# A two-block transformer kernel on one core: the modulation products in wider steps at fixed places, and an attention bias table kept as rows

## The chip, the cores and the metric

The kernel runs on one core of a Trainium2 chip. The core has a matrix engine (TensorE, PE in the profile; its weight loads are PEld), VectorE (DVE), ScalarE (ACT), GpSimd (POOL) and SyncE (SP), which here issues every DMA from one queue, in order. The metric is device time in microseconds for one execution.

## The reference, cut to what matters

`first_block` has two layers. Each takes a vector `mod = silu(c) @ w_ada[li] + b_ada[li]` of 6 x 1024 numbers for the tokens, and the same for the context from `c_ctx`. It is split into a shift, a scale and a gate for the mixer, and a shift, a scale and a gate for the feed-forward part:

```python
m  = unpack(modulate(rms_norm(x, norm1_w[li]), sh1, sc1) @ w_in[li], lb_all[li])
...
x = x + g1 * merge(att, rec, four, w_out[li], dt)
x = x + g2 * conv_ffn(modulate(rms_norm(x, norm2_w[li]), sh2, sc2),
                      w_up[li], conv_w[li], conv_b[li], w_down[li])
```

`second_block` is a gated convolution and then an attention over three groups of heads, with a bias that depends on the distance alone, `bias = bias_tab[bucket]`, in windows of 128 queries by 256 keys:

```python
logits = jnp.where(valid, logits + bias, -jnp.inf)
```

There are 256 tokens and 256 context tokens of width 1024, all in float32.

## The kernel before, in words

Every large product is made of three matmuls per 128 rows of the contraction, on numbers split into a high and a low part. A weight block of 256 columns is fetched as two DMAs of 512 KB into tiles `raw` (`wpart`, L136), rounded to its high part by ScalarE (L138) and to its low part by VectorE (L140). There are three `raw` buffers and two pairs of weight tiles. `gemm` (L160) then forms one product of 128 columns, 24 matmuls over 256 or 512 tokens; `gemm_nat` (L171) forms the transposed kind, 24 matmuls over 256 columns.

The stages follow one another: the start; layer 0's mixer (a gated scan `hgrn`, two halves of an attention `diff_attn`, a Fourier part); its out-projection with `w_out_a` and `w_out_b`; layer 0's feed-forward block (`ffn`: twice 11 pairs of products, then 8 products down), on 512 columns since tokens and context both go on; layer 1 on 256; then the second block.

The modulation vector is wanted in 12 pieces of 1024 columns (banks). The first two of layer 0, the shift and scale of its mixer, are formed at the start. For the other ten, `ada_bank` fetches, for each of eight parts of the contraction, a tile `araw` of 4 x 256 columns (512 KB, L316) and runs four float32 matmuls, each into its own quarter of 32 of the array's columns (L319, 128*32 in the profile). A float32 matmul shows as two records. At the end of a bank `ada_out` copies the sums out, transposes them with PE (L330) and adds the bias. There are three `araw` buffers. The order is not written out by hand: the framework's scheduler places each instruction by a priority, and the table `_ADA` gives each bank an offset by which it stands behind the rest, so that its matmuls fill places where the scheduler finds nothing else:

```python
for a, off in _ADA[li]:
    with self.tc.high_priority(offset=-off):
        self.ada_bank(*a)
```

At the beginning of layer 0's feed-forward block `bias_tables` makes the attention's bias. For each of five window kinds a small matmul (L883) gives, per head, 256 numbers over distance. A DMA (L886) writes them to DRAM as 128 windows of 128, each shifted by one and running backwards: 16 heads x 128 windows x 512 bytes, 1 MB. The attention later reads one head's five windows as a contiguous tile `bt` of 320 KB (L1016). VectorE adds it to the scores (L1136). The query rows are scaled at L1114, and the head outputs leave at L1164.

Of the kernel before, what the change touches and what calls it, by code (L numbers as in the profile page):

```python
# [46 lines left out]
for _n, _w in (("hsel", 32), ("bsel", 512), ("low", 1)):  # L47
# [5 lines left out]
_ADA = ((((0, 2), 800), ((0, 3), 1000), ((0, 4), 1300), ((0, 5), LATER), ((1, 0), LATER), ((1, 1), LATER)),  # L53
        (((1, 2), 500), ((1, 3), 700), ((1, 4), 1200), ((1, 5), LATER)))

# [3 lines left out]
class Builder:  # L59
# [4 lines left out]
    gi = 0  # L64
    keep = {}
# [65 lines left out]
    def wpart(self, W, src, a, b, hold=(None, None)):  # L131
# [4 lines left out]
        nc.sync.dma_start(raw, src.rearrange("p (k c) -> p k c", k=H.shape[1])[:, a:b])  # L136
# [14 lines left out]
    def gemm(self, W, c0, acts, T, t0=0, pt=None, tag=None):  # L151
# [6 lines left out]
        for k, (h, l) in enumerate(acts):  # L158
            for a, c in ((H, h), (H, l), (L, h)):
                nc.tensor.matmul(pt, a[:, k, c0:c0 + P], c[:, t0:t0 + T], start=n == 0, stop=n == tot - 1)  # L160
                n += 1
        return pt

    def gemm_nat(self, W, acts, t0, pt, p0):
# [143 lines left out]
    def ada_bank(self, li, b):  # L308
# [5 lines left out]
        for k in range(KD):  # L314
            raw = self.ring("araw", [P, 4, 256])
            nc.sync.dma_start(raw, d["w_ada"][li, k * P:(k + 1) * P, b * 1024:(b + 1) * 1024]  # L316
                              .rearrange("p (g c) -> p g c", g=4))
            for g in range(4):
                nc.tensor.matmul(pa[32 * g:32 * g + 32, 0:256], self.csil[:, k, :], raw[:, g],  # L319
                                 start=k == 0, stop=k == KD - 1)  # L320
        self.ada_out(li, pa, [b * 8 + g * 2 for g in range(4)], 2)

    def ada_out(self, li, pa, tiles, n):

        nc, mod = self.nc, self.mods[li]
        ad = self.ring("araw", [P, 512])
# [186 lines left out]
    def layer(self, li, states):  # L513
# [29 lines left out]
        for a, off in _ADA[li]:  # L543
            with self.tc.high_priority(offset=-off):
                self.ada_bank(*a)
# [78 lines left out]
        a0 = rec(0, "ps")  # L624
        values()
# [25 lines left out]


# [145 lines left out]
    def ffn(self, li, st2, T):  # L798
# [15 lines left out]
        if li == 0:  # L814
            with self.later():
                self.bias_tables()
        st1 = [dict() for _ in range(ns)]
        hook = self.out_hook(st1[0]) if li == 1 else None
        for half in range(2):
            hid = []  # L820
            for j in range(half * HALF, (half + 1) * HALF):
                w = pre[j] if j in pre else self.wload(d["w_up"][li, j])
# [39 lines left out]
            if cut < 8:  # L862
                ws = [W(m) for m in (6, 7)]
                for v in (1, 0):
                    for m in (6, 7):
                        add(m, v, self.gemm(ws[m - 6], 0, hid, 256, t0=v * 256))
        return st1


    def bias_tables(self):  # L870
# [3 lines left out]
        self.scr = self.dp.tile([16, P, 5, P], F32, name="scr")  # L874
# [5 lines left out]
        for b in range(5):  # L880
# [111 lines left out]
    def attn2(self, st, acts, x):  # L992
# [378 lines left out]
```

## Time and profile before

| | |
|---|---|
| median of three runs | 1778.97 us (1778.38 to 1779.42) |
| profiled execution, its own time | 1775.45 us |
| span of the profiled execution | 1773.6 us |
| mean granted TensorE clock | 0.987 |
| PE busy | 1707.7 us, 96% |
| VectorE, ScalarE, GpSimd busy | 57%, 48%, 18% |
| DMA | 260.64 MB, 147 GB/s on the mean |

The span runs from the first to the last instruction of the profiled execution, and the execution's own time is 1.85 us longer. A busy PE is not one at its peak: a matmul's record includes the time it takes to run out of the array, so that overlapping records are counted once, and a short piece between others carries that time alone. A wait stands in square brackets behind the instruction that followed it, with what ended it.

### The profile page before, as it was taken

The page shows a single profiled execution, that of the slowest core. Times are in us where ns is not written, and L with a number is a line of the kernel's source. Part 1 is how long each engine was busy: PE and PEld are TensorE (multiplying, and loading weights), DVE is VectorE, ACT ScalarE, POOL GpSimd, SP SyncE. Part 2 cuts the span into 40 slices and gives each one's busy share as a digit, 9 for nine tenths or more (in the row PEclk, how much of TensorE's full clock was granted, in tenths as well). Part 3 has the DMA queues.
Part 4 walks back from the last instruction along what each step waited for, and adds up shares of the span by engine and source line. Part 5 has one row for each costly group of instructions (what it writes and reads, how often), then busy time and mean ns, then how long its engine had stood idle before and what let it go on. Part 6 is the DMA issues. An engine that isn't in the chain of part 4 may idle for free.

```text
span 1773.6 us, 29835 instructions
## 1 busy us (share of the span) xinstructions
PE 1707.7 (96%) x11918; PEld 1462.1 (82%) x11918; DVE 1018.5 (57%) x1849; ACT 846.3 (48%) x1481; POOL 320.8 (18%) x412
## 2 busy tenths in 40 slices
PE   6999999987999999989999899999999999999998
PEld 3876766765878888779787799999999999899987
DVE  4557555444543454355865676767666754645656
ACT  4447444334431343253754554665444565545543
POOL 1322210121100011225320210122202203121220
PEclk9999999998999999989999999999999999999999
DMA  9533443576223222344326556555555555444441
GB/s 344 174 108 107 133 133 126 148 125 174 101 69 132 100 95 71 119 150 133 106 86 215 174 165 197 177 176 181 182 185 187 175 186 168 150 142 148 150 144 44
DMA packets 88803, 260.64 MB, mean 147 GB/s; under 512 B 8887, under 2 KB 20535, under 8 KB 88664
## 3 DMA queue, kind: packets, MB, share of 16 engines
q1 hardware_dynamic: 88664, 258.74, 45.6%
q8 instruction: 93, 1.52, 0.3%
q14 instruction: 46, 0.38, 0.1%
HBM read 252.42 MB, written 6.29 MB: 146 GB/s over the span
## 4 chain that ended last, share of the span: by engine, by line
PE 88%; DVE 3%; DMA 3%; ACT 2%; SPq 2%; issue 1%; POOL 0%; ACTq 0%; DVEq 0%
PE pg L160 35%; PE ps L160 15%; PE pu L160 8%; PE ph L160 8%; PE pg L171 7%; PE pa L319 3%; DMA araw<-in_w_ada_dram 2%; PE ps L1129 2%; PE ph L442 1%; PE ps L698 1%; PE pa L1159 1%; PE ph L1155 1%; SPq L316 1%; DVE wL L140 1%; PE pu L736 1%
## 5 line engine op out<-in xcount | busy, mean ns | idle before, releaser
L140 DVE TENSOR_TENSOR wL<-raw,wH 128x1024 fp32r<-128x1024 f32 (+2 forms) x388 | 443.0, 1171 | 254.3 <-ACT wH L138 247.6
L138 ACT CAST wH<-raw 128x1024 fp32r<-128x1024 f32 (+2 forms) x388 | 370.9, 994 | 406.3 <-PE pg L160 157.7
L160 PE MATMUL pg<-hx,wH 128*128 128x256 f32 x1152 | 215.0, 284 | 0.0
L160 PE MATMUL pg<-hm,wH 128*128 128x512 f32 (+1 forms) x736 | 209.7, 366 | 2.8 <-DVE x L657 1.8
L160 PEld LDWEIGHTS pg<-hx,wH 128*128 128x128 f32 x1152 | 178.6, 189 | 5.3 <-issue 4.0
L160 PEld LDWEIGHTS pg<-hm,wH 128*128 128x128 f32 x736 | 130.1, 192 | 42.3 <-issue 13.3
L160 PE MATMUL pg<-hx,wL 128*128 128x256 f32 x576 | 163.1, 283 | 0.0
L160 PE MATMUL pg<-hm,wL 128*128 128x512 f32 (+1 forms) x368 | 132.5, 361 | 0.0
L160 PE MATMUL pg<-h,wH 128*128 128x256 f32 (+1 forms) x464 | 116.1, 339 | 13.2 <-ACT wH L138 11.6
L843 POOL TENSOR_TENSOR tt<-tt 128x512 f32<-128x512 f32 (+1 forms) x44 | 44.7, 1017 | 442.1 <-DVE tt L840 442.1
L160 PE MATMUL ps<-h,wH 128*128 128x256 f32 (+1 forms) x464 | 114.6, 335 | 0.0
L160 PEld LDWEIGHTS pg<-hx,wL 128*128 128x128 f32 x576 | 108.2, 188 | 0.7 <-issue 0.2
L160 PEld LDWEIGHTS pg<-h,wH 128*128 128x128 f32 x464 | 80.7, 193 | 24.0 <-ACT wH L138 12.0
L160 PEld LDWEIGHTS ps<-h,wH 128*128 128x128 f32 x464 | 80.3, 191 | 9.4
L160 PE MATMUL pg<-hid,wH 128*128 128x256 f32 (+1 forms) x360 | 81.6, 318 | 1.1 <-ACT wH L138 1.1
L160 PEld LDWEIGHTS pg<-hm,wL 128*128 128x128 f32 x368 | 70.6, 192 | 14.0 <-issue 5.0
L160 PE MATMUL pg<-h,wL 128*128 128x256 f32 (+1 forms) x232 | 78.2, 337 | 0.0
L160 PE MATMUL ps<-hid,wH 128*128 128x256 f32 (+1 forms) x344 | 78.2, 319 | 0.0
L160 PE MATMUL ps<-h,wL 128*128 128x256 f32 (+1 forms) x232 | 77.6, 334 | 0.0
L319 PE MATMUL pa<-araw,csil 128*32 128x256 f32 x640 | 64.0, 401 | 13.1 <-DMA araw<-in_w_ada_dram 11.5
L187 POOL TENSOR_TENSOR acc<-acc,y 128x256 f32<-128x256 f32 x40 | 37.4, 944 | 205.0 <-ACT y L186 192.9
L160 PE MATMUL pu<-h,wH 128*128 128x256 f32 (+1 forms) x272 | 68.2, 336 | 6.0 <-ACT wH L138 6.0
(408 smaller groups left out, 3866.1 us busy)
## 6 DMA issues: line engine op xcount, KB each, us to landing
raw<-in_w_up_dram SPq DMA_DIRECT2D x88, 512.0 KB, 4.7
araw<-in_w_ada_dram SPq DMA_DIRECT2D x80, 512.0 KB, 5.3
raw<-in_attn_w_in_dram SPq DMA_DIRECT2D x80, 512.0 KB, 4.5
raw<-in_conv_w_in_dram SPq DMA_DIRECT2D x64, 512.0 KB, 4.6
raw<-in_w_in_dram SPq DMA_DIRECT2D x48, 512.0 KB, 4.6
raw<-in_w_down_dram SPq DMA_DIRECT2D x32, 384.0 KB, 3.6
raw<-in_w_down_dram SPq DMA_DIRECT2D x32, 320.0 KB, 2.9
raw<-in_conv_w_out_dram SPq DMA_DIRECT2D x16, 512.0 KB, 4.2
```

Source lines behind the costliest of these rows:

```text
L138: nc.scalar.copy(H[:, a:b], raw)
L140: nc.vector.tensor_tensor(L[:, a:b], raw, H[:, a:b].bitcast(F32), OP.subtract)
L160: nc.tensor.matmul(pt, a[:, k, c0:c0 + P], c[:, t0:t0 + T], start=n == 0, stop=n == tot - 1)
L171: nc.tensor.matmul(pt[:, p0:p0 + 256], c[:, t0:t0 + P], a[:, k, :], start=n == 0, stop=n == tot - 1)
L187: st["last"] = i, (nc.vector if last else nc.gpsimd).tensor_tensor(st["acc"], st["acc"], sq, OP.add)
L316: nc.sync.dma_start(raw, d["w_ada"][li, k * P:(k + 1) * P, b * 1024:(b + 1) * 1024] .rearrange("p (g c) -> p g c", g=4))
L319: nc.tensor.matmul(pa[32 * g:32 * g + 32, 0:256], self.csil[:, k, :], raw[:, g], start=k == 0, stop=k == KD - 1)
L442: nc.tensor.matmul(pt[:, v, c:c + P], l, m, start=True, stop=True)
L698: nc.tensor.matmul(pts[i][:, :n], qa[h][rr, qt * P:(qt + 1) * P], kT[h][rr, k0 * P:k0 * P + n], start=True, stop=True)
L736: nc.tensor.matmul(po[:, 0:P], aT[:, b * P:(b + 1) * P], va[kb // 2][:, kb % 2, hh * P:(hh + 1) * P], start=b == 0, stop=b == nk - 1)
L843: nc.gpsimd.tensor_tensor(tt[1], tt[0], tt[1], OP.mult)
L1129: nc.tensor.matmul(ps[v][:, o:o + ks.stop - ks.start], qh[g][rr[v], i, qs], kh[g][rr[v], i, ks], start=True, stop=True)
```

## The change

The ten later banks are formed in pairs as steps of 2048 columns. A step fetches two `araw` tiles of 2 x 512 columns and runs four matmuls of 512 columns, one per quarter. There are five pairs with eight steps each, 40 steps in place of 80. A step no longer has a low priority. `gemm` and `gemm_nat` call `tick`, and a step is put behind the product that it counts to: behind each product in layer 0's mixer after the first scan's inputs (the pairs 2 and 4 of layer 0), behind each second product in its feed-forward block from the third weight pair on (the pairs 0 and 2 of layer 1), behind each second in layer 1's mixer (pair 4). Each `araw` load is issued behind the latest weight load in the program's order.

The bias table is kept as 16 rows of 5 x 256 numbers, written by one DMA of 80 KB. The shifted windows are made when a tile is read, as 640 runs of 512 bytes that overlap in DRAM. They are not reversed any more. Instead the query rows are written in reversed order in each block of 128, and the head outputs are read reversed.

```diff
-_ADA = ((((0, 2), 800), ((0, 3), 1000), ((0, 4), 1300), ((0, 5), LATER), ((1, 0), LATER), ((1, 1), LATER)),
-        (((1, 2), 500), ((1, 3), 700), ((1, 4), 1200), ((1, 5), LATER)))
...
     def wpart(self, W, src, a, b, hold=(None, None)):
...
-        nc.sync.dma_start(raw, src.rearrange("p (k c) -> p k c", k=H.shape[1])[:, a:b])
+        self.fetch = nc.sync.dma_start(raw, src.rearrange("p (k c) -> p k c", k=H.shape[1])[:, a:b])
...
     def gemm(self, W, c0, acts, T, t0=0, pt=None, tag=None):
...
+        self.tick()
         return pt
...
     def gemm_nat(self, W, acts, t0, pt, p0):
...
+        self.tick()
...
-    def ada_bank(self, li, b):
+    def ada_steps(self, li, b):
...
         for k in range(KD):
-            raw = self.ring("araw", [P, 4, 256])
-            nc.sync.dma_start(raw, d["w_ada"][li, k * P:(k + 1) * P, b * 1024:(b + 1) * 1024]
-                              .rearrange("p (g c) -> p g c", g=4))
+            raw = [self.araw([P, 2, 512]) for _ in range(2)]
+            for i in range(2):
+                c = (b + i) * 1024
+                with self.after(self.fetch):
+                    nc.sync.dma_start(raw[i], d["w_ada"][li, k * P:(k + 1) * P, c:c + 1024]
+                                      .rearrange("p (g c) -> p g c", g=2))
             for g in range(4):
-                nc.tensor.matmul(pa[32 * g:32 * g + 32, 0:256], self.csil[:, k, :], raw[:, g],
+                nc.tensor.matmul(pa[32 * g:32 * g + 32, :], self.csil[:, k, :], raw[g // 2][:, g % 2],
                                  start=k == 0, stop=k == KD - 1)
-        self.ada_out(li, pa, [b * 8 + g * 2 for g in range(4)], 2)
+            if k == KD - 1:
+                self.ada_out(li, pa, [b * 8 + g * 4 for g in range(4)], 4)
+            yield
+
+    def araw(self, shape):
+        return self.lp.tile(shape, F32, name="araw", tag="araw", bufs=3)
+
+    def beside(self, banks, every):
+        self.steps = [self.ada_steps(*b) for b in banks]
+        self.every, self.count = every, 0
+
+    def tick(self):
+        self.count += 1
+        if self.steps and self.count % self.every == 0:
+            self.step()
...
+    def finish_steps(self):
+        while self.steps:
+            self.step()
...
         a0 = rec(0, "ps")
+        self.beside(((0, 2), (0, 4)) if li == 0 else ((1, 4),), 1 if li == 0 else 2)
...
             for j in range(half * HALF, (half + 1) * HALF):
+                if li == 0 and j == 2:
+                    self.beside(((1, 0), (1, 2)), 2)
...
-        self.scr = self.dp.tile([16, P, 5, P], F32, name="scr")
+        self.scr = self.dp.tile([16, 5, 256], F32, name="scr")
...
             nc.scalar.copy(bv[:, b], pt[0:16, 0:256])
-            src = bv[:, b]
-            nc.sync.dma_start(self.scr[:, :, b], bass.AP(tensor=src.tensor, offset=src.offset + 127,
-                                                         ap=[list(src.ap[0]), [-1, P], [1, P]]))
+        nc.sync.dma_start(self.scr, bv)
+
+    def reverse(self, t):
+        n = t.shape[-1] // P
+        return bass.AP(tensor=t.tensor, offset=t.offset + P - 1, ap=[list(t.ap[0]), [P, n], [-1, P]])
...
-            nc.sync.dma_start(t, self.scr[head])
+            row = self.scr[head]
+            nc.sync.dma_start(t, bass.AP(tensor=row.tensor, offset=row.offset, ap=[[1, P], [256, 5], [1, P]]))
```

Four places in the order of instructions follow. Lines of the changed kernel stand some way off: L134 is the weight load, L158 and L170 the products, L320 and L323 the modulation's loads and matmuls, L919 the bias write.

SP's queue around the start of layer 0's feed-forward block, before:

```order
L316 DMA araw<-in_w_ada_dram 128x1024
L886 DMA scr<-bt 2048x1x128
L136 DMA raw<-in_w_up_dram 128x1024
L316 DMA araw<-in_w_ada_dram 128x1024 x5
L886 DMA scr<-bt 2048x1x128 x3
L136 DMA raw<-in_w_up_dram 128x1024
L886 DMA scr<-bt 2048x1x128
L316 DMA araw<-in_w_ada_dram 128x1024 x3
L136 DMA raw<-in_w_up_dram 128x1024 x16
```

and now:

```order
L134 DMA raw<-in_w_up_dram 128x1024 x3
L912 DMA bt<-in_oh_dram 33x1280
L134 DMA raw<-in_w_up_dram 128x1024 x3
L320 DMA araw<-in_w_ada_dram 128x1024 x2
L919 DMA scr<-bt 16x1280
L134 DMA raw<-in_w_up_dram 128x1024 x2
L320 DMA araw<-in_w_ada_dram 128x1024 x2
L134 DMA raw<-in_w_up_dram 128x1024 x2
```

The five writes of 2048 runs, with modulation loads between them, are now one write of 16 rows. The first two loads of the steps that go into the block stand ahead of it.

PE at the end of the out-projection (products `pg<-hm`) and the start of the feed-forward block (`ph<-h`), before:

```order
L160 MATMUL pg<-hm,wL 128x256
L319 MATMUL pa<-araw,csil 32x256 x4
L210 MATMUL pg<-dg,ca 128x128 x2
L883 MATMUL pg<-bt,rb 16x256
L319 MATMUL pa<-araw,csil 32x256 x4
L192 MATMUL ps<-ca,acc 128x1 x2
L883 MATMUL ps<-bt,rb 16x256
L319 MATMUL pa<-araw,csil 32x256 x4
L883 MATMUL pg<-bt,rb 16x256
L319 MATMUL pa<-araw,csil 32x256 x4
L160 MATMUL ph<-h_3431,wH 128x256
L883 MATMUL ps<-bt,rb 16x256
```

and now:

```order
L158 MATMUL pg<-hm,wH 128x256 x2
L158 MATMUL pg<-hm,wL 128x256
L210 MATMUL pg<-dg,ca 128x128 x2
L917 MATMUL pg<-bt,rb 16x256 x2
L192 MATMUL ps<-ca,acc 128x1 x2
L158 MATMUL ph<-h_3230,wH 128x256
L158 MATMUL pg<-h_3230,wH 128x256
L917 MATMUL ps<-bt,rb 16x256 x2
L158 MATMUL ph<-h_3231,wH 128x256
L158 MATMUL ph<-h_3230,wL 128x256
```

The modulation's matmuls between the norm's sums (L192), the spread of its factor (L210) and the bias matmuls have left this place.

PE in layer 0's mixer, where values are formed from the weights `wH` and `wL` by `gemm_nat` (`pg<-wH,hm`, `pg<-wL,hm`), now:

```order
L170 MATMUL pg<-wH,hm 128x256 x2
L170 MATMUL pg<-wL,hm 128x256
L170 MATMUL pg<-wH,hm 128x256
L323 MATMUL pa<-araw,csil 32x512 x2
L170 MATMUL pg<-wH,hm 128x256
L170 MATMUL pg<-wL,hm 128x256
L170 MATMUL pg<-wH,hm 128x256
L323 MATMUL pa<-araw,csil 32x512 x2
```

A step of four matmuls stands here as two pieces of two, three product matmuls apart, since its two tiles are loaded separately.

PE in the feed-forward block, at the end of one weight block's second product (`ph`) and the start of the next, now:

```order
L158 MATMUL ph<-h_3245,wH 128x512
L158 MATMUL ph<-h_3244,wL 128x512
L323 MATMUL pa<-araw,csil 32x512 x4
L158 MATMUL pg<-h_3230,wH 128x512
L158 MATMUL pg<-h_3231,wH 128x512
L158 MATMUL pg<-h_3230,wL 128x512
L158 MATMUL pg<-h_3232,wH 128x512
```

One whole step stands between the products; before, they followed each other directly.

## Rows read from the trace of the kernel before

**Rows 1.** Busy time by engine, from the page: us, share of the span, instructions.

```profile
PE 1707.7 (96%) x11918; PEld 1462.1 (82%) x11918; DVE 1018.5 (57%) x1849; ACT 846.3 (48%) x1481; POOL 320.8 (18%) x412
```

**Rows 2.** Stretches: us, busy us of PE, PEld, DVE, ACT, POOL; clock, DMA share, GB/s.

```profile
45.00:330.00 285.00, 280.80 (x1793) 202.96 (x1792) 162.87 (x377) 145.86 (x322) 55.98 (x82) 1.00 0.39 128
...
424.00:765.00 341.00, 341.00 (x1546) 275.12 (x1544) 158.22 (x211) 120.57 (x169) 37.99 (x31) 1.00 0.30 100
...
800.00:990.00 190.00, 184.46 (x1348) 147.92 (x1346) 121.40 (x264) 99.95 (x202) 48.27 (x74) 1.00 0.44 144
```

**Rows 3.** Chain of waits, layer 0's feed-forward block: start, us, what.

```profile
430.15 5.60 PE ph L160 x24
```

**Rows 4.** Timeline of PE around modulation steps: start, us, instruction, records.

```profile
155.52 1.50 PE L319 MATMUL pa<-araw,csil 128*32 128x256 f32 x24
...
334.32 0.40 PE L160 MATMUL pg<-Qp,wL 128*128 128x512 f32 x1
...
334.64 0.64 PE L319 MATMUL pa<-araw,csil 128*32 128x256 f32 x8
...
335.21 0.51 PE L160 MATMUL pg<-hm,wH 128*128 128x256 f32 x2
...
335.56 0.29 PE L160 MATMUL pg<-hm,wL 128*128 128x256 f32 x1
```

**Rows 5.** Timeline of SP's queue at the start of the feed-forward block.

```profile
365.03 16.86 SPq L886 DMA_DIRECT2D scr<-bt  x3
...
381.94 12.60 SPq L136 DMA_DIRECT2D raw<-in_w_up_dram  x1
...
414.31 10.69 SPq L136 DMA_DIRECT2D raw<-in_w_up_dram  x5
```

**Rows 6.** DMA issues from 335 to 425 us, and two of the stretches there.

```profile
araw<-in_w_ada_dram SPq DMA_DIRECT2D x11, 512.0 KB, 7.2
...
scr<-bt SPq DMA_DIRECT2D x5, 1024.0 KB, 20.1
...
387.00:394.00 7.00, 7.00 (x49) 6.17 (x47) 0.00 (x0) 0.00 (x0) 0.00 (x0) 1.00 0.75 90
...
401.00:408.00 7.00, 2.34 (x5) 1.42 (x6) 2.36 (x3) 3.45 (x4) 0.00 (x0) 0.50 0.83 158
```

**Rows 7.** Timeline of PE at the start of the feed-forward block.

```profile
405.62 1.22 PE L160 MATMUL pg<-h,wH 128*128 128x512 f32 x2 [11.56 <-ACT wH L138]
...
409.69 0.63 PE L160 MATMUL pg<-h,wH 128*128 128x512 f32 x2
...
422.20 1.22 PE L160 MATMUL pu<-h,wH 128*128 128x512 f32 x2 [6.05 <-ACT wH L138]
...
426.49 0.63 PE L160 MATMUL pu<-h,wH 128*128 128x512 f32 x2
```

**Rows 8.** Timeline of PE between out-projection and feed-forward block.

```profile
358.06 1.08 PE L319 MATMUL pa<-araw,csil 128*32 128x256 f32 x8 [4.78 <-DMA araw<-in_w_ada_dram]
...
362.32 0.71 PE L210 MATMUL pg<-dg,ca 128*128 128x128 f32 x4
...
366.89 0.38 PE L160 MATMUL ph<-h,wH 128*128 128x256 f32 x1
```

**Rows 9.** Chain, transposed products in layer 1; DMA issues, 45 to 130 us.

```profile
798.47 20.16 PE pg L171 x171
...
araw<-in_w_ada_dram SPq DMA_DIRECT2D x9, 512.0 KB, 5.8
```

**Rows 10.** Timeline of VectorE at the start of layer 1.

```profile
771.10 0.16 DVE L200 RECIPROCAL rs<-sd 128x2 f32<-128x2 f32 x1
```

**Rows 11.** Bias tiles in the attention: DMA issues, SP's queue, first use on VectorE.

```profile
bt<-scr SPq DMA_DIRECT2D x13, 320.0 KB, 3.0
...
1524.89 2.79 SPq L1016 DMA_DIRECT2D bt<-scr  x2
...
1530.01 0.66 DVE L1136 CUSTOM_DVE_ANT_0 lt<-ps,bt 128x512 f32<-128x512 f32 x1
```

More of the change, by code (lines that the diff above doesn't have):

```diff
@@ L64 @@
     gi = 0
+    steps, every, count = (), 1, 0
     keep = {}
@@ L314, in ada_bank, with step @@
         for k in range(KD):
-            raw = self.ring("araw", [P, 4, 256])
-            nc.sync.dma_start(raw, d["w_ada"][li, k * P:(k + 1) * P, b * 1024:(b + 1) * 1024]
-                              .rearrange("p (g c) -> p g c", g=4))
+            raw = [self.araw([P, 2, 512]) for _ in range(2)]
[4 more added lines that the diff above has]
+                                      .rearrange("p (g c) -> p g c", g=2))
             for g in range(4):
-                nc.tensor.matmul(pa[32 * g:32 * g + 32, 0:256], self.csil[:, k, :], raw[:, g],
+                nc.tensor.matmul(pa[32 * g:32 * g + 32, :], self.csil[:, k, :], raw[g // 2][:, g % 2],
                                  start=k == 0, stop=k == KD - 1)
-        self.ada_out(li, pa, [b * 8 + g * 2 for g in range(4)], 2)
+            if k == KD - 1:
[10 more added lines that the diff above has]
+            self.step()
+    def step(self):
+        while self.steps:
+            try:
+                next(self.steps[0])
+                return
+            except StopIteration:
+                self.steps.pop(0)
+    def finish_steps(self):
+        while self.steps:
+            self.step()
     def ada_out(self, li, pa, tiles, n):
         nc, mod = self.nc, self.mods[li]
-        ad = self.ring("araw", [P, 512])
+        ad = self.araw([P, 512])
         nc.scalar.copy(ad[:, :n * P], pa[:, :n * P])
@@ L542, in layer @@
             self.late_setup()
-        for a, off in _ADA[li]:
-            with self.tc.high_priority(offset=-off):
-                self.ada_bank(*a)
         acts = h
@@ L650, in layer @@
         self.fourier(li, uf, T, mo, fc)
+        self.finish_steps()
         st2 = [dict() for _ in range(ns)]
@@ L815, in ffn @@
             with self.later():
-                self.bias_tables()
+                self.bias_rows()
         st1 = [dict() for _ in range(ns)]
@@ L866, in ffn, with bias_rows @@
                         add(m, v, self.gemm(ws[m - 6], 0, hid, 256, t0=v * 256))
+        self.finish_steps()
         return st1
-    def bias_tables(self):
+    def bias_rows(self):
         nc, d = self.nc, self.d
-        self.scr = self.dp.tile([16, P, 5, P], F32, name="scr")
+        self.scr = self.dp.tile([16, 5, 256], F32, name="scr")
         rb = self.sml("rb", [33, 48], bufs=1)
@@ L1113, in attn2 @@
                     o = self.ring(name, [P, 2, 256])
-                    nc.vector.scalar_tensor_tensor(o.rearrange("p i t -> p (i t)"), raw[n].rearrange("p i t -> p (i t)"),
-                                                   gain, pc, op0=OP.mult, op1=OP.mult)
+                    f = o.rearrange("p i t -> p (i t)")
+                    blocks = lambda t: t.rearrange("p (n t) -> p n t", t=P)
+                    nc.vector.scalar_tensor_tensor(blocks(f) if n else self.reverse(f),
+                                                   blocks(raw[n].rearrange("p i t -> p (i t)")),
+                                                   gain, blocks(pc), op0=OP.mult, op1=OP.mult)
                     to.append(o)
@@ L1163, in values @@
                     y = self.sml("y", [P, 256], bufs=2)
-                    nc.vector.tensor_tensor(y, pavs[i][:, 0:256], sz[:, i], OP.mult)
+                    nc.vector.tensor_tensor(y.rearrange("p (n t) -> p n t", t=P), self.reverse(pavs[i][:, 0:256]),
+                                            sz[:, i].rearrange("p (n t) -> p n t", t=P), OP.mult)
                     u = self.pair("yo", 256, F32R)
@@ L1190, in build @@
             self.lp = e1.enter_context(tc.tile_pool(name="l1", bufs=1))
-            A = dict(araw=3)
             H = dict(hm=16)
@@ L1197, in build @@
             F = ("pg", "ps", "pg", "ps", "pu", "ph")
-            self.phase(K, H, R, N, A)
+            self.phase(K, H, R, N)
             self.gt = M1
@@ L1209, in build @@
             st = self.ffn(0, st, 512)
-            self.phase(K, R, H, N, A)
+            self.phase(K, R, H, N)
             self.gt = M1
```

## The prediction

> **What bounds the kernel now.** I read the page first: TensorE (PE) is busy for 96% of the span [rows 1], so what counts is what PE executes and the few places where it stands still. The stage table comes next: in the first mixer, the first feed-forward block and the second mixer, 816 us together, PE has work in all but 9.7 us [rows 2]. A matmul put into these stretches costs its own time; one taken out gives it back only if other work is ready behind it. The feed-forward pace is 5.60 us per product of 24 matmuls, 0.233 us each [rows 3].
>
> A piece of modulation (matmuls that stand together in PE's order) was priced on the timeline. The eight records of one old step (four matmuls, one per quarter of the array, two passes each) stand between two product matmuls that start at 334.32 and 335.56, 1.24 us apart [rows 4]. Without the step the first would take 0.23 us and the pair that starts at 335.21 would take 0.24, so the step costs 0.77. Three steps together last 1.50 us against 0.64 for one [rows 4], so a further round of the quarters adds 0.43, and 0.34 of a piece is paid for entering and leaving it. A piece of one matmul pays that too: splitting is what is dear.
>
> Then the gaps. At the start of the feed-forward block SyncE's queue (SP) is held: three writes of the bias table hold it for 16.86 us and the weight load behind them for 12.60 [rows 5]. While only the table's writes were moving, the DMA engines were 75% busy and carried 90 GB/s; one such write of 1 MB took a median of 20.1 us to land, a modulation load of 512 KB in this stretch 7.2 [rows 6]. PE waits 11.56 and 6.05 us for weights, and restarts at the lower clock (0.50 granted in that stretch, 1.2 GHz) [rows 6, 7].
>
> **The change part by part.**
>
> *(a) Bias table.* The five writes of 2048 runs of 512 bytes become one of 16 rows of 5 KB, the reversed windows being cut when a tile is read. Both waits go: 17.61 us. With them goes the slow restart: 12 matmuls from 405.62 to 409.69 took 4.07 us where 12 x 0.233 = 2.80 would do, and 9 from 422.20 to 426.49 took 4.29 instead of 2.10 [rows 7], so 1.27 + 2.19. Together 21.1. The five table matmuls stay. What is late next there is a weight load behind two modulation loads; it has a product pair (11.2 us) to land, so I count nothing.
>
> *(b) Out-projection to feed-forward.* PE waits 4.78 us for modulation data here, and the first feed-forward matmul starts at 366.89 [rows 8]. In the new order no modulation is left here. The 96 matmuls of the last out-projection part started at 335.21 [rows 4]; at 0.118 each (20.16 us for 171 [rows 9]) plus 0.4 for the sums they end at 347.0. The norm's chain then shows: from its spread at 362.32 to the first feed-forward matmul 4.57 us passed [rows 8], which gives 351.6 instead of 366.89. That is 15.3, less 2.2 for a restart at the lower clock as in (a): 13. If half the chain is hidden the gain is 17; if the chain is paid twice, 9.
>
> *(c) First mixer.* PE's order had 43 pieces there, 57 rounds: 43 x 0.34 + 57 x 0.43 = 39. Now 16 steps stand in 23 pieces, 24 rounds of 512 columns at 2 x 0.43: 23 x 0.34 + 24 x 0.86 = 28. Of the 11 saved I count 3: many old pieces stood between scores and softmax, where PE had little else ready, and that filler is gone. Against it stands supply. A step needs two loads of 512 KB, and there are three buffers, so the second load of a step is issued only when the step before has released one. Loads took 5.8 us here [rows 9]. Where the products are of 24 x 0.118 = 2.8 us, the values of scan and attention, steps follow at 3.6 us or so with the scan's matmuls, against some 5 to 6 us; the order lets three of them meet this. Each then waits about 2 us: 6, with no loss if the tile's older release covers it and 20 if all eight wait and the clock falls each time. Net of (c): +3.
>
> *(d) First feed-forward block.* 4 pieces of 6 rounds (4 x 0.34 + 6 x 0.43 = 3.9) become 17 pieces of one round: 17 x 1.20 = 20.4. PE has no gap there [rows 2], so the whole difference of 16.5 counts, and 1 for the transposes of two more banks: +17.5. Bounds: 16 if the steps are cheaper at 512 columns, 21 if ScalarE's copies or the transposes hold a product. The copy and the casts have room.
>
> *(e) Second mixer.* 24 pieces with 36 rounds (23.6) become 10 pieces, 12.0. The entry gains almost nothing: the reciprocal for the second spread came only at 771.10 on VectorE [rows 10], behind weight splits, so PE would have waited there without the modulation too. The last seven old pieces, in the out-projection (6.7), are gone outright; some of the others were filler. Of 11.6 I take 8, between 3 and 13.
>
> *(f) Bias tiles and reversals.* Sixteen reads now move 640 runs of 512 bytes. A read took 3.0 us to land [rows 11]; 320 KB at the 90 GB/s of [rows 6] is 3.6 us, so 5 to 6 with the fixed part. The tightest use is 5.1 us after its issue (1524.89 to 1530.01 [rows 11]); others have far more, but weight loads stand behind. I take +2, from 0 to +8. The Trainium skill, DMA: Bandwidth & Descriptors, section Specifications, gives 512 bytes as the size from which a transfer moves at line rate; the trace does not agree for these writes, which keep the engines 75% busy at 90 GB/s. By that rule this term would be 0 and the sum 2 us lower. Twelve VectorE writes and eight reads run backwards, over the same elements; VectorE works beside PE there, so I count nothing.
>
> Sum: -21.1 - 13 + 3 + 17.5 - 8 + 2 = -19.6. The profiled execution took 1775.45 us (span 1773.6), 0.2% below the median of 1778.97; so 1755.8 against it, and **1759.4** as a median. The columns themselves bring little: it is stalls that go, and the feed-forward block pays for part of it.
>
> **The rivals.**
>
> *Nothing is lost where I gave filler away.* The mixers' other work closes up and tiles are in time: (c) brings -8 instead of +3 and (e) -13, so 1743. For it: PE idles only 9.7 us in three large stages, so products are plentiful. Against: pieces between score matmuls in the first mixer.
>
> *Late tiles in the first mixer.* All eight steps among the short products wait 2 us, with the clock falling: 20 instead of 6, so 1773. For it: three buffers for two loads a step and a single queue. Against: the DMA engines are only 39% busy there [rows 2].
>
> *Slower: SP's queue is blocked by the steps.* In the feed-forward block a modulation load waits for PE to release a tile, and every weight load behind it waits too. From the issue of a weight load at 414.31 [rows 5] to the first matmul on it at 422.20 [rows 7] pass 7.9 us. A product pair and a step give 12.4. The point of decision is therefore 4.5 us of delay per step: beyond it each of 15 steps costs PE the excess and a restart at the lower clock, 2. With 0.5 of excess that is 2.5 a step, 37 in all, so 1797. For it: the order puts the second of each pair of loads ahead of the weights, and that load carries the wait. Against: casts are two buffers ahead.
>
> *The table moves its cost instead of losing it.* If the 512-byte reads of the attention part delay weights by their 2 x 2.5 us per pair of heads' tiles, six times, 30 come back: 1787. The read buffers and weights in flight speak against this.
>
> **How the numbers follow.** The forecast (1750 to 1767) gets 0.52, the better case 0.20, late tiles 0.14, the two slower mechanisms 0.09, and 0.05 is left for a net of nothing. A measurement of this kernel tells differences from about 0.2%, 3.6 us. Late tiles together with the upper bounds of (d) and (f) reach no change, which is where 0.02 of it lies. So: faster 0.84, same 0.07, slower 0.09. The range 1741 to 1773 takes in the better case and the late tiles, and leaves out the slower ones and a gain above 38.
>
> **What would show it.** Right: no wait over 2 us on PE between the out-projection and the third feed-forward weight; feed-forward products at 5.60 with a step of about 1.2 after every second; modulation's busy time near 48 to 52 instead of 64; SP free of any issue over 10 us that is put down to the table. (c) shows as PE's idle time on modulation data in the first mixer: 6 expected. Wrong: products slower than 5.60 in the feed-forward block, a step that costs over 1.5 us there, waits on bias tiles by VectorE, or new gaps in front of weights.

## The result, and the profile after

The changed kernel took 1756.93 us (median; 1752.95 to 1757.33) against 1778.68 (1777.32 to 1779.42) for the kernel before on the same chip: a ratio of 0.9871, 95% interval 0.9852 to 0.9891. It is 1.3% faster. The forecast was 1759.4 us with a range of 1741 to 1773, and faster with a chance of 0.84. Two repeats on other chips gave 0.9882 (0.9868 to 0.9895) and 0.9886 (0.9869 to 0.9902). A fourth execution, the one that was profiled, took 2144.02 us at a mean granted clock of 0.718 and is left out of this comparison, so the profile below is that of the first repeat, e1: its own time is 1753.84, its span 1751.9.

The spans differ by 21.7 us, and the profile shows stage by stage where they come from. Both kernels are cut at the same events: the first product of the first mixer behind its norm, the first matmul of its out-projection, the first matmul of the feed-forward block, and then the first spread of each norm (layer 1, its feed-forward block, the convolution block, the attention). The windows view of the kernel before; columns as in [rows 2]:

```profile
51.52:335.21 283.69, 280.96 (x1786) 203.26 (x1786) 160.86 (x369) 143.45 (x317) 53.49 (x79) 1.00 0.38 126
335.21:366.89 31.68, 25.06 (x192) 17.68 (x188) 16.04 (x36) 12.86 (x30) 8.54 (x12) 0.89 0.74 201
366.89:766.44 399.55, 381.86 (x1818) 310.12 (x1815) 179.84 (x256) 139.59 (x198) 50.30 (x46) 0.98 0.37 106
766.44:988.63 222.19, 212.65 (x1518) 169.16 (x1517) 141.52 (x305) 117.21 (x236) 61.74 (x92) 0.98 0.44 148
988.63:1201.76 213.13, 209.26 (x1713) 207.96 (x1714) 148.21 (x241) 123.02 (x204) 31.85 (x43) 0.98 0.54 172
1201.76:1429.82 228.06, 227.78 (x1899) 227.58 (x1898) 154.95 (x231) 107.45 (x149) 45.75 (x50) 1.00 0.55 182
1429.82:1773.60 343.78, 335.06 (x2789) 308.39 (x2787) 192.79 (x347) 180.19 (x306) 59.31 (x72) 1.00 0.43 140
```

The same of the changed kernel (e1):

```profile
50.57:337.06 286.49, 279.83 (x1620) 200.51 (x1621) 158.07 (x360) 143.08 (x317) 50.41 (x81) 0.99 0.34 114
337.06:356.26 19.20, 15.89 (x115) 13.56 (x114) 16.13 (x34) 12.68 (x28) 8.46 (x12) 1.00 0.19 64
356.26:751.36 395.10, 395.07 (x1897) 310.48 (x1896) 182.07 (x258) 140.95 (x201) 50.85 (x47) 1.00 0.39 129
751.36:966.09 214.73, 201.05 (x1376) 163.59 (x1377) 140.19 (x299) 114.67 (x233) 63.98 (x92) 0.97 0.40 133
966.09:1180.09 214.00, 210.12 (x1713) 208.72 (x1714) 148.22 (x237) 123.13 (x204) 31.85 (x43) 0.98 0.53 172
1180.09:1408.15 228.06, 227.78 (x1899) 227.58 (x1898) 154.99 (x231) 107.38 (x149) 45.52 (x50) 1.00 0.54 181
1408.15:1751.90 343.75, 335.06 (x2789) 308.37 (x2787) 192.85 (x347) 180.24 (x306) 59.24 (x72) 1.00 0.43 140
```

Read the first number behind each window. The first mixer is 2.8 us longer, the way to the feed-forward block 12.5 shorter, the feed-forward block 4.5 shorter, the second mixer 7.5 shorter; the rest differs by less than 1. In the feed-forward block PE is now busy for 395.07 of 395.10 us, where it stood still for 17.7 before.

The timeline of SP's queue in e1 at the start of that block, to be held against [rows 5]:

```profile
356.83 0.33 SPq L134 DMA_DIRECT2D raw<-in_w_up_dram  x1
357.21 0.90 SPq L320 DMA_DIRECT2D araw<-in_w_ada_dram  x2
358.46 0.33 SPq L919 DMA_DIRECT2D scr<-bt  x1
```

The table's one write holds the queue for 0.33 us; three of the old writes held it for 16.86. The chain of waits in the middle of the block, which was a plain row of 5.60 [rows 3]:

```profile
419.49 0.99 PE pa L323 x8
420.49 5.79 PE pg L158 x24
426.28 5.60 PE ps L158 x24
431.88 0.99 PE pa L323 x8
```

A step and a pair of products take 431.88 - 419.49 = 12.39 us. Two products are 11.20, so a step is 1.19: 0.99 of its own, and some 0.2 by which the product behind it is longer.

### The profile page after: what moved, and what is told of

It reads as the page before. It is cut to its first block, busy times and chain, and to the rows that moved or that the text cites. A ratio compares the mean times of both kernels' runs of the same rounds, so it can differ in the third digit from the quotient of the medians.

```text
span 2142.2 us, 29173 instructions
## 1 busy us (share of the span) xinstructions
PE 2099.1 (98%) x11598; PEld 1681.0 (78%) x11598; DVE 1019.2 (48%) x1829; ACT 845.3 (39%) x1474; POOL 316.4 (15%) x412
## 4 chain that ended last, share of the span: by engine, by line
PE 96%; DVE 1%; DMA 1%; ACT 1%; issue 0%; SPq 0%; POOL 0%; DVEq 0%; ACTq 0%; POOLq 0%
PE pg L158 38%; PE ps L158 16%; PE pg L170 8%; PE pu L158 8%; PE ph L158 8%; PE pa L323 3%; PE ph L473 2%; PE ps L728 2%; PE ps L1171 2%; PE pa L1201 1%; PE pu L766 1%; PE ph L1197 1%; PE pg L819 1%; PE pa L303 1%; DVE wL L138 1%; PE pu L759 1%
## 5 line engine op out<-in xcount | busy, mean ns | idle before, releaser
L158 PE MATMUL pg<-hm,wH 128*128 128x512 f32 (+1 forms) x736 | 252.2, 429 | 3.6 <-ACT hm L394 2.1
L158 PE MATMUL pg<-hx,wH 128*128 128x256 f32 x1152 | 251.9, 315 | 0.0
L158 PEld LDWEIGHTS pg<-hx,wH 128*128 128x128 f32 x1152 | 213.4, 225 | 6.4 <-issue 5.8
L158 PEld LDWEIGHTS pg<-hm,wH 128*128 128x128 f32 x736 | 143.9, 213 | 75.6 <-issue 30.9
L158 PE MATMUL pg<-hx,wL 128*128 128x256 f32 x576 | 180.5, 313 | 0.0
L158 PE MATMUL pg<-hm,wL 128*128 128x512 f32 (+1 forms) x368 | 157.9, 429 | 0.0
L158 PE MATMUL pg<-h,wH 128*128 128x256 f32 (+1 forms) x464 | 140.1, 392 | 1.7 <-ACT h L394 1.4
L158 PE MATMUL ps<-h,wH 128*128 128x256 f32 (+1 forms) x464 | 138.5, 391 | 0.0
L158 PEld LDWEIGHTS pg<-hx,wL 128*128 128x128 f32 x576 | 128.3, 223 | 0.8 <-issue 0.4
L158 PEld LDWEIGHTS pg<-h,wH 128*128 128x128 f32 x464 | 91.8, 219 | 29.4 <-ACT wH L136 8.3
L158 PEld LDWEIGHTS ps<-h,wH 128*128 128x128 f32 x464 | 92.1, 220 | 21.7 <-issue 4.2
L158 PE MATMUL pg<-hid,wH 128*128 128x256 f32 (+1 forms) x360 | 97.7, 363 | 1.0 <-ACT wH L136 1.0
L158 PEld LDWEIGHTS pg<-hm,wL 128*128 128x128 f32 x368 | 78.7, 214 | 24.9 <-issue 8.5
L170 PE MATMUL pg<-wH,hm 128*128 128x256 f32 x384 | 92.9, 332 | 0.0
L158 PE MATMUL ps<-hid,wH 128*128 128x256 f32 (+1 forms) x344 | 92.7, 364 | 0.0
L158 PE MATMUL ps<-h,wL 128*128 128x256 f32 (+1 forms) x232 | 91.6, 395 | 0.0
L158 PE MATMUL pg<-h,wL 128*128 128x256 f32 (+1 forms) x232 | 91.3, 394 | 0.0
L170 PEld LDWEIGHTS pg<-wH,hm 128*128 128x128 f32 x384 | 75.5, 235 | 12.4 <-issue 8.9
L170 PE MATMUL pg<-wH,hx 128*128 128x256 f32 x384 | 85.0, 313 | 0.0
```

## The experiments

The changed kernel is called "after" here. Ratios are to the kernel before on the same chip, with 95% intervals.

**e1: after, for the profile.** No edit.

> The changed kernel once more, for an undisturbed profile. By the prediction's terms its stages stand to those of before (first mixer 285 us, out-projection to feed-forward 37, feed-forward 398, second mixer 225) as: first mixer 282 to 290 with about 6 us of PE idle on modulation data; PE's way from out-projection to first feed-forward matmul 13 us shorter; feed-forward about 21 shorter for the bias table's stall and 17.5 longer for its steps; second mixer 8 shorter; attention 0 to 8 longer. Rivals: late tiles show as 20 us idle in the first mixer; the case in which nothing is lost shows as a first mixer 8 and a second mixer 13 shorter. Total 1753 to 1760.

Measured: 1755.68 us. The stages stand as forecast, but one part of the forecast is not there: in the first mixer PE waits for modulation data only once, for 0.2 us. This is what stands there instead, from PE's timeline:

```profile
198.64 1.12 PE L728 MATMUL ps<-ka,qa 64*128 64x512 f32 x2 [1.29 <-ACT e L734]
...
212.82 0.66 PE L759 MATMUL pu<-ca,e 128*128 128x128 f32 x4 [1.22 <-DVE mx L733]
...
215.49 1.16 PE L766 MATMUL pu<-va,aT 128*128 128x128 f32 x8 [2.01 <-ACT aT L761]
```

All three are waits on softmax, and all come after the mixer's last step, which was done at 181 us.

**e2 and e3: one part of the change alone.** e2 is the kernel before with the bias rows and reversals, its modulation untouched. e3 is after with the old table and without the reversals:

```diff
-                self.bias_rows()
+                self.bias_tables()
...
-            nc.sync.dma_start(t, bass.AP(tensor=row.tensor, offset=row.offset, ap=[[1, P], [256, 5], [1, P]]))
+            nc.sync.dma_start(t, self.scr[head])
```

> Before with the bias rows alone, modulation as it was. Theory (terms a and f of the prediction): the stall at the start of the feed-forward block, 21.1 us, goes, and the attention pays 2, so 19 us faster than before, about 1757 to 1760: nearly the whole gain of the change. Rival 1 (the stall was only partly the table's; the old modulation loads fill the queue there): 8 to 12 us faster. Rival 2 (the bias reads of 512-byte runs cost 10 us or more in the attention): 10 us faster or less, with the attention stage longer than 273 us.

> Before with the modulation steps alone, bias tables as they were. Theory (terms b to e: -13 +3 +17.5 -8): no change within 3 us, 1776 to 1782. Rival 1 (the steps themselves bring the gain, as the mixers close up): 10 to 20 us faster, 1759 to 1769. Rival 2 (steps in the feed-forward block and the table's writes block each other in SP's queue): 5 us slower or more.

Measured: e2 1757.58 us, ratio 0.9898 (0.9883 to 0.9913); e3 1771.27, ratio 0.9967 (0.9955 to 0.998). The bias rows alone bring 19.0 of the 20.9 us of e1, the number of e2's first theory. In the trace of e2 the feed-forward block and the second mixer are:

```profile
364.81:743.15 378.34, 378.34 (x1821) 308.24 (x1820) 179.44 (x252) 139.52 (x197) 49.70 (x47) 1.00 0.31 102
743.15:970.26 227.11, 214.63 (x1509) 168.76 (x1508) 142.40 (x309) 118.53 (x239) 61.60 (x92) 0.97 0.44 143
```

The block is 21.2 us shorter than before, and the old second mixer, which this edit does not touch, 4.9 longer: PE idles 2.9 us more in it and its modulation takes 22.09 us instead of 20.39, presumably since the scheduler has placed it elsewhere. The first feed-forward matmul comes 2.1 us earlier. The 2 us that the theory gave to the attention are not there (343.42 instead of 343.78), so that the sum comes to 19 is in part luck. Both theories of e3 were off: the modulation steps alone bring 5.3 us, not 0 and not 10 to 20. The trace shows part of it: with the old table and the new steps PE waits once,

```profile
409.70 1.22 PE L158 MATMUL pu<-h,wH 128*128 128x512 f32 x2 [13.29 <-ACT wH L136]
```

13.29 us where the kernel before waits 17.61 in two pieces [rows 7]. Part of the table's stall thus went with the old modulation loads that shared its stretch, and the two parts of the change are not quite additive: 19.0 and 5.3 apart, 20.9 together.

**e4: no late tiles.** One pair of loads per bank, reused by all its steps:

```diff
-            raw = [self.araw([P, 2, 512]) for _ in range(2)]
-            for i in range(2):
+            if k == 0:
+                raw = [self.araw([P, 2, 512]) for _ in range(2)]
+            for i in range(2 if k == 0 else 0):
```

> The changed kernel with one pair of loads per bank: all eight steps of a bank multiply the tile of its first step, and the loads of the other seven are left out, so that no step but the first waits for data. Theory (c: about 6 us of waiting for late tiles in the first mixer, none in the other stages): 4 to 9 us faster than the changed kernel, all of it in the first mixer, about 1748 to 1753. Rival 1 (no tile is late; other transfers aren't held up either): no change, within 2 us. Rival 2 (the loads hold up weights in SP's queue in all three stages): 15 us faster or more, and the gain spread over the stages.

Measured: 1754.63 us, ratio 0.9878 (0.9863 to 0.9894), against 0.9882 of after. In the whole time the loads cost nothing that can be measured. From the first spread of the first norm to that of the feed-forward norm, e4 and then e1:

```profile
24.48:348.96 324.48, 313.36 (x1852) 224.99 (x1851) 182.54 (x418) 159.22 (x351) 68.29 (x100) 0.99 0.25 83
```

```profile
22.10:351.87 329.77, 317.85 (x1852) 225.53 (x1851) 182.56 (x418) 161.56 (x353) 64.69 (x100) 0.98 0.38 129
```

The stretch is 5.3 us shorter (e5, e9 and e11, with the same steps there as e1, lie between 327.69 and 330.80), and the feed-forward block, 402.81 instead of 399.49, gives 3.3 of it back. But PE's idle time is almost the same, 11.12 and 11.92 us, so the gain is not that of waits for late tiles. My theory of late tiles fell, and with it the rival "Late tiles in the first mixer".

**e5: no steps in the feed-forward block.**

```diff
-                    self.beside(((1, 0), (1, 2)), 2)
+                    self.mods.append(self.cp.tile([P, 2, 48], F32, name="mod1"))
+                    self.nc.vector.memset(self.mods[1], 0.25)
```

> The changed kernel without the 16 modulation steps in layer 0's feed-forward block: the first four sixths of layer 1's modulation are a constant instead (neither loaded nor multiplied). Theory (term d: PE has no gap there, so a step costs its own time and nothing else; in the changed kernel a pair of products with its step takes 12.4 us against 2 x 5.60, so 1.20): 16 x 1.20 = 19.2 and about 1 for transposes, so 19 to 21 us faster than the changed kernel, 1735 to 1737, all between the spread of the feed-forward norm and that of layer 1's norm. Rival 1 (the steps' 16 MB of loads also hold up weights): 25 us faster or more. Rival 2 (weights bound the products, and the steps fill waits): 12 us faster or less, with new waits on weights.

Measured: 1736.15 us, ratio 0.9769 (0.9753 to 0.9786), 19.5 below after: the theory's 19 to 21. From norm to norm the block takes 379.92 us instead of 399.49, so it is all there. (Neither e5 nor e8 ran beside after on one chip; by the ratios e5 lies 20.1 us below it.)

**e6: narrow matmuls in the same pieces.**

```diff
-            for g in range(4):
-                nc.tensor.matmul(pa[32 * g:32 * g + 32, :], self.csil[:, k, :], raw[g // 2][:, g % 2],
-                                 start=k == 0, stop=k == KD - 1)
+            for c in (0, 256):
+                for g in range(4):
+                    nc.tensor.matmul(pa[32 * g:32 * g + 32, c:c + 256], self.csil[:, k, :],
+                                     raw[g // 2][:, g % 2, c:c + 256],
+                                     start=k == 0 and c == 0, stop=k == KD - 1 and c == 256)
```

> Each step as two rounds of four matmuls of 256 columns, in one piece, instead of one round of 512; loads, buffers and places are the same. Theory (0.34 for a piece and 0.43 for every 256 columns, whatever their grouping): no change, within 2 us of the changed kernel. Rival 1 (each round has a fixed cost of its own, so width is what saves): 0.2 to 0.3 more per step, 40 steps, so 8 to 12 us slower than the changed kernel. Rival 2 (narrow rounds overlap better): 4 us faster or more.

Measured: 1762.79 us, but the four runs lie between 1757.83 and 1766.40; ratio 0.9918 (0.9891 to 0.9945). The time speaks for the first rival, the trace does not. Chain of waits in the feed-forward block of e6:

```profile
420.52 1.00 PE pa L324 x16
421.52 5.79 PE pg L158 x24
```

Sixteen records of 256 columns take 1.00 us where eight of 512 took 0.99, and the product behind is the same. So in this stretch the price of a step is that of its columns, as the theory has it. The profiled run was the fastest of the four; where the others lost up to 8 us no trace shows, and this stays open; the interval of e6 overlaps that of after in e9 (0.9869 to 0.9902).

**e7 and e10: every second product in the first mixer.**

```diff
-        self.beside(((0, 2), (0, 4)) if li == 0 else ((1, 4),), 1 if li == 0 else 2)
+        self.beside(((0, 2), (0, 4)) if li == 0 else ((1, 4),), 2)
```

> In the first mixer a step behind every second product instead of behind each. In the changed kernel the last step there is done at 181 us; at 199, 213 and 215 us PE then waits 4.5 us on softmax and the clock is 0.83 from 200 to 210. Theory (what the first mixer lost is filler: steps that come later fill these waits): 3 to 6 us faster than the changed kernel. Rival 1 (the steps don't fall into the waits): same within 2 us. Rival 2 (the steps left over at the mixer's end stand in a row and each waits some 5 us for its loads): 8 us slower or more.

> The changed kernel once more, beside the next run on the same chip. Every theory: as before, 0.987 to 0.989 of the kernel before.

> Once more the kernel with a step behind every second product in the first mixer. Theory (the first mixer gains some 5 us of filled waits, and part is given back where PE happens to restart at the lower clock at the feed-forward block): 2 to 5 us faster than the changed kernel on the same chip. Rival (what was seen was chance): within 1.5 us of it.

Measured: e7 1752.94 us, ratio 0.9866 (0.9846 to 0.9885), and e10 the same ratio, with 1752.99; e9, the changed kernel beside e10, 1756.69 and 0.9886 (0.9869 to 0.9902). Twice some 3 us faster than after, with intervals that overlap: likely the better version, not proven. From the first spread of the first norm to that of the feed-forward norm e10 takes 8.1 us less than e1 (and 9.2 less than e9):

```profile
22.21:343.86 321.65, 313.31 (x1853) 223.78 (x1851) 184.66 (x418) 159.84 (x351) 65.46 (x100) 0.99 0.39 132
```

PE idles 8.34 us of it instead of 11.92, and waits on softmax for 2.0 us instead of 5.8; the clock of 0.99 instead of 0.98 is worth some 3 us more (an estimate from the two rows). The rest is not accounted for. But e10 gives back 2.0 in the feed-forward block and 3.3 in the second mixer. The first can come from the clock. PE stands still for 2.05 us between out-projection and feed-forward block in each of these kernels; in e1:

```profile
355.26 0.60 PE L917 MATMUL pg<-bt,rb 33*16 33x256 f32 x2 [2.05 <-ACT bt L918]
```

Behind it the granted clock falls to the lower level, 1.2 GHz, for a stretch that differs: some 3 us in e1, 7 in e9 and 10 in e10. Granted clock around that restart (the figure ahead of the last two), e1:

```profile
345.00:365.00 20.00, 17.82 (x123) 15.40 (x122) 15.76 (x37) 13.18 (x30) 12.71 (x16) 0.91 0.28 85
```

e10:

```profile
345.00:365.00 20.00, 17.95 (x103) 14.79 (x103) 14.46 (x31) 11.58 (x24) 12.97 (x16) 0.74 0.27 84
```

Counted from the norm's spread, at 351.87 and 343.86, 20 us give the same 0.91 and 0.74. That is 3.4 us of work, more than the 2.0. e9, the same program as e1, had 0.83 there, and its block took 401.05 us, 1.6 longer than that of e1 and 0.4 shorter than that of e10: stage times of one execution are good to a few us only.

**e8: no steps in the first mixer.**

```diff
-        self.beside(((0, 2), (0, 4)) if li == 0 else ((1, 4),), 1 if li == 0 else 2)
+        if li == 0:
+            self.nc.vector.memset(self.mods[0][:, :, 16:48], 0.25)
+        else:
+            self.beside(((1, 4),), 2)
```

> The changed kernel without the 16 steps in the first mixer: the last four sixths of layer 0's modulation are a constant instead (neither loaded nor multiplied). Theory (term c: a step costs its own time, 23 pieces and 24 rounds of 512 columns, 28 us; no tile is late): 25 to 30 us faster than the changed kernel, 1726 to 1731. Rival 1 (part of the steps is filler, and without them PE waits on scan and softmax and restarts at the lower clock): 10 to 20 us faster. Rival 2 (their 16 MB of loads hold up weights as well): over 32 us faster.

Measured: 1745.48 us, ratio 0.9818 (0.9799 to 0.9838), 10.2 below after (11.4 by the ratios). Rival 1 holds: 16 steps that keep PE busy for 26.2 us cost some 10 to 11. The trace of e8 from the first norm's spread to the feed-forward norm's:

```profile
23.68:338.95 315.27, 296.37 (x1716) 226.41 (x1715) 182.82 (x408) 160.36 (x351) 69.92 (x100) 0.96 0.24 79
```

PE idles 18.9 us of it; in e1 it idles 11.9 in the same stretch, at a clock of 0.98. In their own stretch the steps cost 14.5 us (329.77 to 315.27): of the 26.2, 7.0 come back as idle time, and the lower clock takes some 6 (an estimate from 0.96 and 0.98). Without the steps the feed-forward block is 3.4 longer and the second mixer 2.0, which is about the difference between 14.5 and 10. So in the mixer a good part of a step is filler; in the feed-forward block (e5) none is: 16 steps cost 19.5 there.

**e11: a step behind every product in the feed-forward block.**

```diff
-                    self.beside(((1, 0), (1, 2)), 2)
+                    self.beside(((1, 0), (1, 2)), 1)
```

> In the first feed-forward block a step behind every product instead of behind every second, 16 steps in the first half of the block. This is the rival in which the steps block SP's queue, at twice the rate: a step's 1 MB and a product's 0.25 MB of weights must come in 5.60 + 1.20 = 6.8 us, 184 GB/s where the first mixer moved 128 and the feed-forward block 128 on the mean. Theory (the queue has room, a step costs 1.20 wherever it stands): same as the changed kernel within 3 us. Rival (a load that waits for a free tile holds the weights behind it): products wait, 15 us slower or more, with waits on weights of 2 us or more per step.

Measured: 1771.67 us, ratio 0.9963 (0.995 to 0.9976), 15.0 above after on the same chip (e9). The loss has the rival's size and not its cause: PE waits for no weight, although SP's queue is held for up to 12.03 us by five loads of modulation in a row. PE's timeline in e11 shows what happens:

```profile
411.84 1.05 PE L323 MATMUL pa<-araw,csil 128*32 128x512 f32 x4
412.82 0.73 PE L158 MATMUL pg<-h,wH 128*128 128x512 f32 x2
413.39 0.40 PE L158 MATMUL pg<-h,wL 128*128 128x512 f32 x1
413.62 0.40 PE L158 MATMUL pg<-h,wH 128*128 128x512 f32 x1
413.95 1.05 PE L323 MATMUL pa<-araw,csil 128*32 128x512 f32 x4
```

Most steps are cut in two: two matmuls (four records), some of the product, the other two. The scheduler does this when it sets the order; why it does stays open. At the pace of after all steps but one stand whole. Each half takes 1.05 us, as long as all four matmuls take together. The windows view of L323 alone, from norm to norm, first e1, then e11:

```profile
351.87:751.36 399.49, 18.09 (x128) 1.00 0.38 128
```

```profile
351.90:767.73 415.83, 31.38 (x128) 0.99 0.38 123
```

As many records, 13.3 us more; with 0.2 for each of 12 further pieces (29 instead of 17) that is 15.7 of the 16.3 us by which the stage is longer than in e1 (14.8 longer than in e9). The Trainium skill, TensorEngine Tiling (Array Packing), section Tiling Modes, has both halves of this: independent tiles of the array can run in parallel, and a change of tiling mode drains TensorE. The trace agrees with the first: half a round of quarters takes as long as a whole one. That the product behind a step takes 5.79 us instead of 5.60 fits the second; no run here shows the drain by itself.

**e12: the old table's writes from another queue.** The kernel before, with one word changed:

```diff
-            nc.sync.dma_start(self.scr[:, :, b], bass.AP(tensor=src.tensor, offset=src.offset + 127,
+            nc.gpsimd.dma_start(self.scr[:, :, b], bass.AP(tensor=src.tensor, offset=src.offset + 127,
```

> Before, with the five writes of the bias table issued from GpSimd's queue instead of SP's; the writes themselves, 2048 runs of 512 bytes each, are the same. Theory 1 (term a: it is SP's queue that the writes hold, and the weights stand behind them): PE's two waits of 11.56 and 6.05 us shrink to 5 in sum or less, 10 to 18 us faster than before. Theory 2 (it is the DMA engines that the short runs fill, whatever queue they come from, and weights share them): the waits stay within 5 us of what they were, and the time within 5 us of before. Theory 3 (GpSimd is held in SP's place, and the norm's products on it come late): as slow as before or slower, with new waits on GpSimd.

Measured: 1775.38 us, ratio 0.999 (0.9981 to 0.9999). In time it is theory 2, in waits it lies between theories 1 and 2. DMA queues and issues from 335 to 425 us in e12:

```profile
q0 software_dynamic: 1360, 5.24, 54.4%
...
scr<-bt POOLq DMA_DIRECT2D x5, 1024.0 KB, 26.8
raw<-in_w_up_dram SPq DMA_DIRECT2D x8, 512.0 KB, 11.1
```

SP's queue is rid of the writes, and the weights still take 11.1 us to land, where after takes 5.0 in the same stretch. PE's wait there:

```profile
414.70 1.22 PE L160 MATMUL pu<-h,wH 128*128 128x512 f32 x2 [8.87 <-ACT wH L138]
```

8.87 us, and 0.53 a little later, instead of 17.61. So the other queue takes away about half of the wait. What remains is not a delay on GpSimd: the cast that ends PE's wait had itself waited for its weights, and the slowest weight load of this stretch took 30.7 us to land:

```profile
413.61 1.04 ACT L138 CAST wH<-raw 128x1024 fp32r<-128x1024 f32 x1 [18.65 <-DMA raw<-in_w_up_dram]
```

It fits with DMA engines that the table's writes fill whatever queue they come from: over these 90 us the writes take 54.4% of the 16 engines' time (the row of q0). The move changed one thing more: the same 5.24 MB show as 1360 packets, where the kernel before has 10240 packets of 512 bytes to 2 KB in this stretch. A wait of 2.3 us on the norm's output, which VectorE forms, is new. From norm to norm the block is 6.3 us shorter (397.81 for 404.12), and the second mixer takes them back (228.12 for 222.19), as in e2. The bias rows, one write of 16 long runs, take the whole wait away (in e2 PE is busy for all of the 378.34 us).

## Why the prediction was right, point by point

- **(a) Bias table, -21.1.** From the first feed-forward matmul to layer 1's norm, e2 takes 378.34 us and the kernel before 399.55: -21.2. Both waits and both slow restarts of [rows 7] are gone. The sum had a slip: from 405.62 to 409.69 the trace has nine matmuls, as in the second stretch, and not 12, so that restart cost 1.97 and not 1.27, and the term would be 21.8. The reason was too narrow: freeing SP's queue alone takes away only half of the wait (e12).
- **(b) Out-projection to feed-forward, -13.** 31.68 became 19.20: -12.5. The way there is not quite the forecast one, as PE's timeline of e1 shows:

```profile
337.06 0.40 PE L158 MATMUL pg<-hm,wH 128*128 128x256 f32 x2
...
347.53 0.50 PE L192 MATMUL ps<-ca,acc 128*128 128x1 f32 x4
...
351.87 0.61 PE L210 MATMUL pg<-dg,ca 128*128 128x128 f32 x4
...
356.26 0.36 PE L158 MATMUL ph<-h,wH 128*128 128x256 f32 x1
```

  From spread to first matmul 4.39 us, where [rows 8] gave 4.57. But the spread comes 14.8 us after the start, where the forecast had 11.8 (335.21 to 347.0): between the 96 matmuls stand two waits of 0.35 and 0.78 us, other small matmuls, and short pauses. The 2.2 us for a restart at the lower clock were not spent here, where the granted clock is 1.00; the lower clock came behind the first matmuls of the block (0.66 from 356.87 to 361.87). Two errors of some 3 and 2 us cancel, so that the term is met this closely is luck.
- **(c) First mixer, +3.** Measured +2.8, by other means, so the size is luck. Late tiles were to cost 6 and cost 0.2 (e1; for e4 see there): the step that failed is "Each then waits about 2 us". A step's matmuls were placed where their data were there: PE had other work until then. The 23 pieces of the forecast are in the trace. In e1 eight of the 16 steps are cut; in e4, without the loads, still six or seven (19 pieces), so most of the cuts in the mixer are not made by the loads, and the reason given with the order of instructions ("since its two tiles are loaded separately") does not hold for them. The windows view of the modulation's matmuls, before and after:

```profile
51.52:335.21 283.69, 31.29 (x298) 1.00 0.38 126
```

```profile
50.57:337.06 286.49, 26.19 (x128) 0.99 0.34 114
```

  5.1 us fewer of modulation, where the forecast saved 11 (39 to 28); the products beside the pieces add some 0.7 to it (0.13 for each of 41 pieces, 0.77 less 0.64 [rows 4], against 0.2 for each of 23; an estimate). Against it 3.9 more of PE's idle time (283.69 - 280.96 = 2.73 became 6.66), the waits on softmax above, and 1.7 for a restart at the lower clock at 200 us, where four us ran at 0.57. That gives +0.5; 2.3 are not accounted for. That part of what was taken out was filler ("Of the 11 saved I count 3") is in line with e8, which tests the new steps and not the old pieces.
- **(d) First feed-forward block, +17.5.** 395.10 in e1 against 378.34 in e2: +16.8. A step costs 1.19, the forecast 1.20; the loads hold up nothing at this pace (e5). The rival "SP's queue is blocked by the steps" did not come: even at twice the pace of steps, with SP held for 12 us by loads of modulation, PE still had its weights (e11).
- **(e) Second mixer, -8.** 222.19 to 214.73: -7.5. Ten pieces, busy for 12.34 us; forecast 12.0. PE is busy for 11.6 us less, the 11.6 of the forecast, and idle for 4.1 more (9.54 and 13.68), so some of the old pieces were filler here too.
- **(f) Bias tiles, +2.** The attention takes 343.75 us and took 343.78: 0. DMA issues in the attention of e1:

```profile
bt<-scr SPq DMA_DIRECT2D x13, 320.0 KB, 4.3
```

  The reads land in 4.3 us where they took 3.0 [rows 11]; I had 5 to 6. The rule of the Trainium skill, DMA: Bandwidth & Descriptors, section Specifications, would have put this term at 0, and 0 it was. But the trace does not agree with the rule itself: a read is 1.3 us slower in runs of 512 bytes; it is hidden, not free.

Sum of what was forecast -19.6, of the spans -21.7. Of the signs named, products at 5.60 us with a step of 1.2, and the queue free of long issues for the table, are there. Two are missed: modulation's busy time is 56.6 us, not 48 to 52; and PE has one wait over 2 us, the 2.05 on ScalarE's copy for the table (e10). "The table moves its cost instead of losing it" falls with (f). Of "Nothing is lost where I gave filler away" nothing came: the first mixer got longer, not 8 us shorter, and the second gained 7.5, not 13.

## What to carry to other kernels

A filler's price depends on where it stands: 16 steps cost 19.5 us in a stretch that PE fills by itself, and 14.5 (10 in the whole time) in one that waits on other engines, although half of them were cut in two there; so put them there first. A group of small matmuls that share the array should stay in one piece, since half a group costs as much as the whole; look in the trace whether the scheduler has cut it. A write of many short runs is better made fewer and longer than moved to another queue, which saved only part of its stall and hardly any time (1775.38 us for 1776.93).

## What was not expected of the hardware

- Two matmuls on two quarters of the array take 1.05 us, exactly what four on four take; in 29 pieces instead of 17 the same 16 steps made their stage 16.3 us longer than in e1.
- The same restart, after the same wait of 2.05 us, had a mean granted clock over 20 us of 0.91 in one execution and 0.83 in another of the same program; the stage behind it took 399.49 and 401.05 us from norm to norm.
- A write that left SP's queue for GpSimd's still went with late weights on SP's: they took 11.1 us to land, more than the 7.5 they took in the kernel before.
